# A decoder block's feed-forward entry: h2's evacuation split between ScalarE and VectorE, Silu's table loaded earlier, two sums moved from POOL to VectorE and placed later

## The chip, the cores and the metric

The kernel runs on one core of a Trainium2 chip. The metric is the device time of one execution in microseconds (us), the median of several runs. Engines are named as in the profile: PE is the matmul engine, DVE is VectorE, ACT is ScalarE, POOL is GpSimd, SP is the engine whose queue issues the DMAs.

## What is computed

The reference is one decoder block over 512 tokens of width 1024: two attention mixers, a merge through `w_out`, then a gated feed-forward network. Only its end is touched here:

```
x  = x + gt1 * (merged @ w_out)
h2 = rms_norm(x, norm2_gain) * (1.0 + sc2) + sh2
x  = x + gt2 * ((silu(h2 @ ffn_w_gate) * (h2 @ ffn_w_up)) @ ffn_w_down)
```

`sc2`, `sh2`, `gt1` and `gt2` are rows of `silu(c) @ ada_w + ada_b`. The feed-forward width is 2816, that is 22 columns of 128. All is in float32.

## The kernel before, in words

**Precision.** Each matmul operand is split in a high half (rounded to the matmul's format by a copy on ACT, `hi_of`) and a low half (source minus high half, `lo_of`, on DVE unless another engine is named). A product is then three matmuls: high by high, high by low, low by high. A weight chunk of 128x1024 (`wchunk`) is one DMA into `raw`, one ACT instruction into `whi` and one DVE subtraction into `wlo`; each of these three has four buffers.

**Order.** The program is written as generators that are stepped in an order chosen by hand (`mix`, `steps`, `run`). A scheduler then fixes the queue of each engine when the kernel is built: among instructions whose inputs are ready in its timing model it takes the one that is written first. A queue is executed strictly in its order. The class `Paced` wraps each engine; while its `gate` is set, each of its instructions is also ordered behind the gate's instruction by the scheduler, without a semaphore. All instructions of the wrapped engines carry line 144 in the profile, so groups are told apart by their tiles.

**Around the change.** `out_pairs` (L1344) computes the second half of `w_out`, for two token tiles at a time; `use_o` (L1330) adds the result to the residual `x2` on DVE and squares it on ACT (`junk`). `make_h2(q)` (L1365) handles half `q` of the tokens, 256 of them: a row of small DVE instructions for the reciprocal root (`rsqrt`), the scaled rows `xs`, and then for each pair of the eight columns `k` of h2 four PE transposes into one PSUM bank `pt` (there are two such banks) and, per column, the scale and shift out of PSUM into `h2f`, the high half `h2h` and the low half `h2l`. The low halves of odd columns are on POOL.

`first_gate_up` (L1567) multiplies the first pair of weight columns: for each half of the tokens four slabs of 24 matmuls of 256 tokens, gate (`fg`), up (`fu`), gate, up; all four accumulators (`mm`, four PSUM banks) are held to the end. `make_h2(1)` is stepped between the slabs of the first half. Then `gu_finish` (L1430) applies Silu to the gate accumulators on ACT, and multiplies with the up ones on DVE. `finish_mid` (L1419) splits the result into `mh` and `ml` for the down projection.

The second pair of columns (`gate_up(2)`, L1551) is plain: two gate slabs and two up slabs of 24 matmuls of 512 tokens. From the third pair on the gate product is done with seven products of half size in place of eight (`seven_products`, accumulators `fx` and `fy`). These need sums and differences of blocks of h2, the tiles T1 to T4, each with a high and a low half, made once in `h2_sums` (L1445) in two steps `j`, and sums of weight blocks (`weight_sums`, L1466, tiles `s3` and `s24`) for every pair. T1 to T4 are built in place in `h2f`.

Between the slabs the last rows of `ada_w` are worked off in portions (`mods_gen`): a strip is loaded by SP into a single buffer and two multiply-adds on DVE (`macc`) consume it.

At the end of the entry the lines L1590 to L1597 stand in this order: two gate chunks of the second pair into the list `early`, `gu_finish`, the first step of the sums, one up chunk into `early`, the rest of the sums, `finish_mid` for the first pair. `plain` (L1544) takes its chunks from `early` while there are any.

Of the kernel before, what the change touches and what calls it, by code (L numbers as in the profile page):

```python
# [14 lines left out]
AF = mybir.ActivationFunctionType  # L15
ALU = mybir.AluOpType
# [4 lines left out]
P = 128  # L21
# [3 lines left out]
KD = D // P  # L25
# [89 lines left out]
def hybrid_block(ctx, tc, a, out):  # L115
# [42 lines left out]
    def hi_of(dst, src, scale=1.0):  # L158
        act.activation(out=dst, in_=src, func=AF.Copy, scale=scale)

    def lo_of(dst, src, hi, eng=None):
        (eng or dve).tensor_tensor(out=dst, in0=src, in1=f32v(hi), op=ALU.subtract)
# [13 lines left out]
    ones = cst.tile([P, P], F32, name="ones")  # L176
# [77 lines left out]
    def wchunk(src, parts, n, eng_lo=None, cut=1):  # L254
        raw = wp.tile([P, 1024], F32, name="raw", tag="raw")
        rv = raw[:, : parts * n].rearrange("p (a n) -> p a n", a=parts)
        sp.dma_start(out=rv, in_=src)
        h = wp.tile([P, 1024], F32R, name="whi", tag="whi")
        l = wp.tile([P, 1024], F32R, name="wlo", tag="wlo")
        m = parts * n // cut  # L260
        for i in range(cut):
            c = slice(i * m, (i + 1) * m)
            hi_of(h[:, c], raw[:, c])
            lo_of(l[:, c], raw[:, c], h[:, c], eng_lo)
        return (h[:, : parts * n].rearrange("p (a n) -> p a n", a=parts),
                l[:, : parts * n].rearrange("p (a n) -> p a n", a=parts))

    def rows(w, r0, parts, c0, n):
        return w[r0 : r0 + parts * P, c0 : c0 + n].rearrange("(a p) n -> p a n", p=P)
# [15 lines left out]
    def run(gen):  # L285
        for _ in gen:
            pass
# [25 lines left out]
    def mix(*pairs):  # L313
        todo = [[g, n, 0] for g, n in pairs if n]
        while todo:
            best = min(todo, key=lambda e: (e[2] + 0.5) / e[1])
            if next(best[0], "end") == "end":
                todo.remove(best)
            else:
                best[2] += 1  # L320
                yield
# [22 lines left out]
    def gemm_tok(A, w, kt, c0, n, consume, tag="", eng_lo=None):  # L344
        ps = [mm.tile([P, S], F32, name=f"g{tag}{t}", tag="mm") for t in range(NT)]
        for k0 in range(0, kt, 2):
            parts = min(2, kt - k0)
            h, l = wchunk(rows(w, k0 * P, parts, c0, n), parts, n, eng_lo)
            for i in range(parts):
                k = k0 + i  # L350
                for t in range(NT):
                    ah, al = A(k, t)
                    pe.matmul(ps[t][:, :n], ah, h[:, i, :], start=(k == 0), stop=False)
                    pe.matmul(ps[t][:, :n], ah, l[:, i, :], start=False, stop=False)
                    pe.matmul(ps[t][:, :n], al, h[:, i, :], start=False, stop=(k == kt - 1))
            yield
        for t in range(NT):
            consume(t, ps[t][:, :n])
            yield
# [426 lines left out]
    def part(gen, n):  # L786
        for _ in range(n):
            if next(gen, "end") == "end":
                return
            yield  # L790
# [169 lines left out]
    mods_gen = mods()  # L960
# [369 lines left out]
    def use_o(c):  # L1330
        cs = slice(c * S, (c + 1) * S)

        def f(t, ps):
            tm = hp2.tile([P, S], F32, name="tm", tag="tm", bufs=2)
            dve.tensor_tensor(out=tm, in0=ps, in1=gt[4][:, cs], op=ALU.mult)
            dve.tensor_tensor(out=x2[t][:, cs], in0=x2[t][:, cs], in1=tm, op=ALU.add)
            junk = hp2.tile([P, S], BF16, name="junk", tag="junk", bufs=2)
            act.activation(out=junk, in_=x2[t][:, cs], func=AF.Square, accum_out=s2[:, c, t : t + 1])
        return f
# [25 lines left out]
    def make_h2(q):  # L1365
        need_mod(3)
        ts = slice(2 * q, 2 * q + 2)
        tcol = slice(2 * q * P, (2 * q + 2) * P)
        v = s2[:, 0, ts]
        dve.tensor_tensor(out=v, in0=v, in1=s2[:, 1, ts], op=ALU.add)  # L1370
        dve.tensor_scalar(out=v, in0=v, scalar1=1.0 / D, scalar2=EPS, op0=ALU.mult, op1=ALU.add)
        rsqrt(r2[:, ts], v, hp2, f"x2{q}")
        xs = [hp2.tile([P, D], F32, name="xs", tag="xs", bufs=4) for _ in range(2)]
        for t in (2 * q, 2 * q + 1):
            if t % 2 == 0:
                dve.tensor_scalar(out=xs[t % 2], in0=x2[t], scalar1=r2[:, t : t + 1], scalar2=None, op0=ALU.mult)
            else:
                act.activation(out=xs[t % 2], in_=x2[t], func=AF.Copy, scale=r2[:, t : t + 1])
        yield
        for k0 in range(0, KD, 2):  # L1380
            pt = tp.tile([P, 2, 2, P], F32, name="pt", tag="tp")
            for i in range(2):
                for j in range(2):
                    pe.transpose(pt[:, i, j, :], xs[j][:, (k0 + i) * P : (k0 + i + 1) * P], ident)
            for i in range(2):
                k = k0 + i
                h2 = h2f[k // 2][:, k % 2, tcol]
                dve.tensor_scalar(out=h2, in0=pt[:, i].rearrange("p a b -> p (a b)"), scalar1=modc[:, 3, k : k + 1],
                                  scalar2=modc[:, 2, k : k + 1], op0=ALU.mult, op1=ALU.add)
                hi_of(h2T[k][0][:, tcol], h2)  # L1390
                lo_of(h2T[k][1][:, tcol], h2, h2T[k][0][:, tcol], pool if k % 2 else dve)
            yield

    wo = gemm_tok(mA, a["w_out"][0], KD, 0, S, use_o(0), tag="wo0")
    steps(wo, 2)
    need_mod(4)
# [22 lines left out]
    def finish_mid(f0, sg, up=None):  # L1419
        mh = midp.tile([P, 2, S], F32R, name="mh", tag="mh")  # L1420
        ml = fp.tile([P, 2, S], F32R, name="ml", tag="ml", bufs=4)
        for i in [slice(0, 2)] if up is None else range(2):
            if up is not None:
                dve.tensor_tensor(out=sg[:, i], in0=sg[:, i], in1=up[i], op=ALU.mult)
            hi_of(mh[:, i], sg[:, i])
            lo_of(ml[:, i], sg[:, i], mh[:, i])
        for i in range(2):
            mid[f0 + i] = (mh[:, i], ml[:, i])
# [16 lines left out]
    def h2_sums():  # L1445
        def both(nm):
            return [h2s.tile([P, 4, 256], F32R, name=f"{nm}{e}") for e in "hl"]

        T1, T2, T3, T4 = (both(f"T{i}") for i in range(1, 5))
        for j in range(2):  # L1450
            b1, b2 = h2f[j], h2f[2 + j]
            jj = slice(2 * j, 2 * j + 2)
            dve.tensor_tensor(out=b1[:, :, LO], in0=b1[:, :, HI], in1=b1[:, :, LO], op=ALU.subtract)
            split_into([v[:, jj] for v in T1], b1[:, :, LO])
            pool.tensor_tensor(out=b1[:, :, HI], in0=b2[:, :, HI], in1=b1[:, :, HI], op=ALU.subtract)
            dve.tensor_tensor(out=b2[:, :, HI], in0=b2[:, :, HI], in1=b1[:, :, LO], op=ALU.subtract)
            split_into([v[:, jj] for v in T2], b2[:, :, HI])
            pool.tensor_tensor(out=b2[:, :, LO], in0=b2[:, :, LO], in1=b2[:, :, HI], op=ALU.subtract)
            split_into([v[:, jj] for v in T4], b2[:, :, LO])
            split_into([v[:, jj] for v in T3], b1[:, :, HI])  # L1460
            yield
        sums.update(T1=T1, T2=T2, T3=T3, T4=T4)
# [76 lines left out]
        dve.tensor_tensor(out=g[:, 1, LO], in0=A, in1=d, op=ALU.add)  # L1539
        yield g  # L1540

    early = []

    def plain(nm, w, f0):  # L1544
        ps = {(nm, i): mm.tile([P, S], F32, name=f"f{nm}{i}", tag="mm") for i in range(2)}
        for k0 in range(0, KD, 4):
            hl = early.pop(0) if early else wchunk(rows(w, k0 * P, 4, f0 * P, 256), 4, 256)
            gu_matmuls(ps, nm, k0, hl, slice(0, S), True)
            yield ps

# [36 lines left out]
    h2s = ctx.enter_context(tc.tile_pool(name="h2s", bufs=1, reuse_waits="tile"))  # L1587
    fp = ctx.enter_context(tc.tile_pool(name="fp", bufs=1, side="right", reuse_waits="tile"))
    strip_src["pool"] = fp
    for k0 in range(0, KD, 4):  # L1590
        early.append(wchunk(rows(wg, k0 * P, 4, 2 * P, 256), 4, 256))
    sg_first = gu_finish(0, ps_first)
    sums_gen = h2_sums()
    next(sums_gen)
    early.append(wchunk(rows(wu, 0, 4, 2 * P, 256), 4, 256))
    run(sums_gen)
    finish_mid(0, sg_first)  # L1597

    def store(c, t, ps):
        cs = slice(c * S, (c + 1) * S)  # L1600
# [33 lines left out]
    for i, (f0, f1) in enumerate(parts):  # L1634
        for f in range(f0, f1, 2):
            if f > 0:
                run(mix((gate_up(f), 6), (part(mods_gen, 4), 4)))
        if i == 0:
            run(mods_gen)
            need_mod(5)  # L1640
        down(f0, f1, i == len(parts) - 1)
# [25 lines left out]
```

## Time and profile before

| what | value |
|---|---|
| median of 3 runs | 907.83 us (907.36 to 909.1) |
| the profiled execution | 906.09 us |
| its span in the profile | 904.0 us |
| PE busy | 855.2 us, 95% |
| DVE busy | 636.0 us, 70% |
| ACT busy | 432.4 us, 48% |
| POOL busy | 176.3 us, 20% |
| granted clock of PE, mean | 0.983 of full speed; 1.00 from 490 us on |

The span is what the trace covers; the time is measured around it. Starts in the rows are us from the start of the span. A timeline row has the start, the duration, the engine, the line, the operation, the tile it writes and those it reads, the count, and in brackets the idle time of the engine before it with what ended that. Instructions of one engine overlap a little, so starts of neighbours are closer together than their durations.

### The profile page before, as it was taken

What the parts mean: (1) busy time and instruction counts of PE and PEld (TensorE: products, weight loads), DVE (VectorE), ACT (ScalarE), POOL (GpSimd) and SP (SyncE); (2) the same over time, 40 slices, a digit from 0 to 9 for tenths busy, and PEclk for the clock granted to TensorE, in tenths of its full rate; (3) what the DMA queues carried; (4) which work ended last, traced back from release to release, by engine and by line L of the source; (5) the groups of instructions that cost most, each with busy time, mean ns of one, the idle gap of its engine ahead of it and who ended that gap; (6) DMA issues with size and microseconds to landing.
All of it is one profiled execution on the core that took longest, in us unless ns stands there. A gap on an engine that the chain in (4) does not pass through costs nothing.

```text
span 904.0 us, 13055 instructions
## 1 busy us (share of the span) xinstructions
PE 855.2 (95%) x4676; PEld 731.4 (81%) x4676; DVE 636.0 (70%) x1288; ACT 432.4 (48%) x863; POOL 176.3 (20%) x222
## 2 busy tenths in 40 slices
PE   5999899899999997999999989999999999999997
PEld 4879899677777786787777878888899889988986
DVE  5857786778976788578779898866754565555644
ACT  5335654787764644466654345341344224431440
POOL 0003335434432037231148014000000000000000
PEclk9999999999999999699999999999999999999999
DMA  9934445321100654135488671553233313342312
GB/s 317 303 98 130 138 140 140 82 71 46 49 12 24 213 150 140 58 106 152 154 293 287 213 229 43 168 163 94 69 106 121 103 53 112 94 119 91 94 47 94
DMA packets 98116, 115.48 MB, mean 128 GB/s; under 512 B 6548, under 2 KB 70660, under 8 KB 98052
## 3 DMA queue, kind: packets, MB, share of 16 engines
q1 hardware_dynamic: 97956, 114.62, 41.3%
q8 instruction: 37, 0.61, 0.3%
q14 instruction: 27, 0.22, 0.1%
q10 hardware_dynamic: 96, 0.03, 0.0%
HBM read 106.24 MB, written 8.39 MB: 127 GB/s over the span
## 4 chain that ended last, share of the span: by engine, by line
PE 73%; DVE 13%; DMA 7%; ACT 2%; issue 2%; SPq 1%; POOL 1%; DVEq 0%; POOLq 0%; ACTq 0%
PE d L144 14%; PE fu L144 13%; PE gp L144 9%; PE fx L144 6%; PE ga L144 5%; PE fy L144 4%; PE pt L144 4%; PE av L144 3%; DMA raw<-in_ada_w_dram 3%; PE fg L144 3%; PE wa L144 2%; DVE macc L144 2%; PE gwo L144 2%; DVE wlo L144 2%; PE ps L144 2%
## 5 line engine op out<-in xcount | busy, mean ns | idle before, releaser
L144 ACT ACTIVATE whi<-raw 128x1024 fp32r<-128x1024 f32 (+4 forms) x162 | 142.1, 892 | 183.0 <-PE d L144 57.8
L144 DVE TENSOR_TENSOR wlo<-raw,whi 128x1024 fp32r<-128x1024 f32 (+3 forms) x122 | 144.0, 1184 | 73.5 <-ACT whi L144 73.1
L144 PE MATMUL fu<-h2l,whi 128*128 128x512 f32 (+1 forms) x192 | 71.3, 372 | 0.0
L144 PE MATMUL fu<-h2h,whi 128*128 128x512 f32 (+1 forms) x192 | 70.7, 372 | 0.0
L144 PE MATMUL fu<-h2h,wlo 128*128 128x512 f32 (+1 forms) x192 | 69.9, 373 | 0.0
L144 PE MATMUL d<-whi,mh 128*128 128x512 f32 x176 | 69.8, 398 | 0.0
L144 PE MATMUL d<-wlo,mh 128*128 128x512 f32 x176 | 69.6, 395 | 0.0
L144 PE MATMUL d<-whi,ml 128*128 128x512 f32 x176 | 67.0, 394 | 0.0
L144 ACT ACTIVATE s<-s,mn 128x384 f32<-128x384 f32 (+2 forms) x96 | 52.5, 548 | 23.0 <-DVE mn L144 22.3
L144 DVE TENSOR_TENSOR plo<-pt,phi 128x512 fp32r<-128x512 f32 (+2 forms) x78 | 46.1, 601 | 21.5 <-ACT phi L144 21.1
L144 POOL TENSOR_TENSOR wlo<-raw,whi 128x512 fp32r<-128x512 f32 x40 | 52.3, 1329 | 44.4 <-ACT whi L144 44.4
L144 PE MATMUL gp<-hTh,whi 128*128 128x512 f32 x128 | 55.4, 433 | 3.7 <-ACT qn L144 3.7
L144 ACT ACTIVATE phi<-pt 128x512 fp32r<-128x512 f32 (+2 forms) x78 | 40.1, 526 | 31.8 <-PE pt L144 31.4
L144 PE MATMUL gp<-hTh,wlo 128*128 128x512 f32 x128 | 52.0, 406 | 0.0
L144 PE MATMUL gp<-hTl,whi 128*128 128x512 f32 x128 | 51.6, 404 | 0.0
L144 DVE SCALAR_TENSOR_TENSOR macc<-raw,csil,macc 128x512 f32<-128x512 f32 x45 | 37.1, 829 | 8.8 <-DMA raw<-in_ada_w_dram 8.3
L144 PEld LDWEIGHTS fu<-h2l,whi 128*128 128x128 f32 x192 | 36.2, 189 | 6.1
L144 PEld LDWEIGHTS fu<-h2h,whi 128*128 128x128 f32 x192 | 35.9, 189 | 6.0
L144 PEld LDWEIGHTS fu<-h2h,wlo 128*128 128x128 f32 x192 | 35.6, 189 | 5.5
L144 PEld LDWEIGHTS d<-whi,mh 128*128 128x128 f32 x176 | 33.0, 188 | 8.2 <-issue 0.2
L144 PEld LDWEIGHTS d<-whi,ml 128*128 128x128 f32 x176 | 33.0, 188 | 8.1
L144 PEld LDWEIGHTS d<-wlo,mh 128*128 128x128 f32 x176 | 33.0, 188 | 7.9 <-issue 0.2
(427 smaller groups left out, 2427.6 us busy)
## 6 DMA issues: line engine op xcount, KB each, us to landing
raw<-in_ada_w_dram SPq DMA_DIRECT2D x26, 512.0 KB, 4.3
raw<-in_ffn_w_gate_dram SPq DMA_DIRECT2D x22, 512.0 KB, 4.7
raw<-in_ffn_w_up_dram SPq DMA_DIRECT2D x22, 512.0 KB, 3.8
raw<-in_ffn_w_down_dram SPq DMA_DIRECT2D x22, 512.0 KB, 4.9
araw<-in_ada_w_dram SPq DMA_DIRECT2D x32, 256.0 KB, 6.3
raw<-in_w_in_dram SPq DMA_DIRECT2D x16, 512.0 KB, 3.9
spill<-gs SPq DMA_DIRECT2D x24, 256.0 KB, 2.0
raw<-in_w_in_dram SPq DMA_DIRECT2D x12, 352.0 KB, 3.2
```

What stands on the lines that cost most here:

```text
L144: out = call(*args, **kw)
```

## The change

Four edits, all between `w_out` and the third pair of weight columns.

In `make_h2` an even column's high half is written by ACT straight from PSUM (Identity with scale and bias columns), while DVE writes its float32 value from the same bank; an odd column's float32 value is written by ACT from PSUM and its high half copied from that. All low halves are on DVE.

Ahead of `w_out` a Silu of one column is put on ACT, ordered behind ACT's last instruction so far, the last high half of the merged rows `mTh`.

In `h2_sums` the two subtractions per step that were on POOL are on DVE. Its two steps no longer follow `gu_finish`: they stand behind the first and second slab of the second pair, and DVE and ACT may take them only behind that slab's last matmul. The call of `finish_mid` for the first pair follows the third slab, and the portions of `mods_gen` of this pair come after it.

The list `early` is gone: the second pair's chunks are made where its slabs use them.

```
@@ -1385,12 +1385,21 @@
             for i in range(2):
                 k = k0 + i
                 h2 = h2f[k // 2][:, k % 2, tcol]
-                dve.tensor_scalar(out=h2, in0=pt[:, i].rearrange("p a b -> p (a b)"), scalar1=modc[:, 3, k : k + 1],
-                                  scalar2=modc[:, 2, k : k + 1], op0=ALU.mult, op1=ALU.add)
-                hi_of(h2T[k][0][:, tcol], h2)
-                lo_of(h2T[k][1][:, tcol], h2, h2T[k][0][:, tcol], pool if k % 2 else dve)
-            yield
-
+                src = pt[:, i].rearrange("p a b -> p (a b)")
+                a2, b2 = modc[:, 3, k : k + 1], modc[:, 2, k : k + 1]
+                hi, lo = (v[:, tcol] for v in h2T[k])
+                if i == 0:
+                    act.activation(out=hi, in_=src, func=AF.Identity, scale=a2, bias=b2)
+                    dve.tensor_scalar(out=h2, in0=src, scalar1=a2, scalar2=b2, op0=ALU.mult, op1=ALU.add)
+                else:
+                    act.activation(out=h2, in_=src, func=AF.Identity, scale=a2, bias=b2)
+                    hi_of(hi, h2)
+                lo_of(lo, h2, hi)
+            yield
+
+    act.gate = act.last
+    act.activation(out=warm, in_=ones[:, 0:1], func=AF.Silu)
+    act.gate = None
     wo = gemm_tok(mA, a["w_out"][0], KD, 0, S, use_o(0), tag="wo0")
     steps(wo, 2)
     need_mod(4)
@@ -1452,10 +1461,10 @@
             jj = slice(2 * j, 2 * j + 2)
             dve.tensor_tensor(out=b1[:, :, LO], in0=b1[:, :, HI], in1=b1[:, :, LO], op=ALU.subtract)
             split_into([v[:, jj] for v in T1], b1[:, :, LO])
-            pool.tensor_tensor(out=b1[:, :, HI], in0=b2[:, :, HI], in1=b1[:, :, HI], op=ALU.subtract)
+            dve.tensor_tensor(out=b1[:, :, HI], in0=b2[:, :, HI], in1=b1[:, :, HI], op=ALU.subtract)
             dve.tensor_tensor(out=b2[:, :, HI], in0=b2[:, :, HI], in1=b1[:, :, LO], op=ALU.subtract)
             split_into([v[:, jj] for v in T2], b2[:, :, HI])
-            pool.tensor_tensor(out=b2[:, :, LO], in0=b2[:, :, LO], in1=b2[:, :, HI], op=ALU.subtract)
+            dve.tensor_tensor(out=b2[:, :, LO], in0=b2[:, :, LO], in1=b2[:, :, HI], op=ALU.subtract)
             split_into([v[:, jj] for v in T4], b2[:, :, LO])
             split_into([v[:, jj] for v in T3], b1[:, :, HI])
             yield
@@ -1539,12 +1548,10 @@
         dve.tensor_tensor(out=g[:, 1, LO], in0=A, in1=d, op=ALU.add)
         yield g
 
-    early = []
-
     def plain(nm, w, f0):
         ps = {(nm, i): mm.tile([P, S], F32, name=f"f{nm}{i}", tag="mm") for i in range(2)}
         for k0 in range(0, KD, 4):
-            hl = early.pop(0) if early else wchunk(rows(w, k0 * P, 4, f0 * P, 256), 4, 256)
+            hl = wchunk(rows(w, k0 * P, 4, f0 * P, 256), 4, 256)
             gu_matmuls(ps, nm, k0, hl, slice(0, S), True)
             yield ps
 
@@ -1587,14 +1594,13 @@
     h2s = ctx.enter_context(tc.tile_pool(name="h2s", bufs=1, reuse_waits="tile"))
     fp = ctx.enter_context(tc.tile_pool(name="fp", bufs=1, side="right", reuse_waits="tile"))
     strip_src["pool"] = fp
-    for k0 in range(0, KD, 4):
-        early.append(wchunk(rows(wg, k0 * P, 4, 2 * P, 256), 4, 256))
     sg_first = gu_finish(0, ps_first)
     sums_gen = h2_sums()
-    next(sums_gen)
-    early.append(wchunk(rows(wu, 0, 4, 2 * P, 256), 4, 256))
-    run(sums_gen)
-    finish_mid(0, sg_first)
+
+    def gated_sums():
+        dve.gate = act.gate = pe.last
+        next(sums_gen, None)
+        dve.gate = act.gate = None
 
     def store(c, t, ps):
         cs = slice(c * S, (c + 1) * S)
@@ -1634,7 +1640,13 @@
     for i, (f0, f1) in enumerate(parts):
         for f in range(f0, f1, 2):
             if f > 0:
-                run(mix((gate_up(f), 6), (part(mods_gen, 4), 4)))
+                slabs = gate_up(f)
+                if f == 2:
+                    for _ in range(3):
+                        next(slabs)
+                        gated_sums()
+                    finish_mid(0, sg_first)
+                run(mix((slabs, 6), (part(mods_gen, 4), 4)))
         if i == 0:
             run(mods_gen)
             need_mod(5)
```

## Rows read from the trace of the kernel before

**Rows 1.** Waits of PE, 490 us to the end: total, times, longest.
```profile
PE fg L144 <- DVE h2l L144: 2.4, 2, 2.2
PE fg L144 <- ACT sg L144: 1.9, 1, 1.9
PE pt L144 <- DVE h2f L144: 1.7, 1, 1.7
```

**Rows 2.** Windows; columns: stretch, length, then busy us of each engine.
```profile
561.70:586.00 24.30, 22.38 (x100) 18.36 (x99) 19.88 (x25) 10.83 (x14) 2.21 (x1) 1.00 0.62 189
586.00:904.00 318.00, 313.37 (x1720) 271.15 (x1718) 184.83 (x253) 104.89 (x138) 0.00 (x0) 1.00 0.32 97
```

**Rows 3.** Timeline of PE: start, duration, group, [idle before it <-releaser].
```profile
536.70 0.39 PE L144 MATMUL fg<-h2l,whi 128*128 128x256 f32 x1 [2.24 <-DVE h2l L144]
...
559.28 0.28 PE L144 MATMUL fg<-h2h,wlo 128*128 128x256 f32 x1
...
563.63 0.50 PE L144 MATMUL fg<-h2h,whi 128*128 128x512 f32 x1 [1.92 <-ACT sg L144]
```

**Rows 4.** Timeline of VectorE, the first half of the tokens' h2.
```profile
531.77 1.89 DVE L144 TENSOR_SCALAR h2f<-pt,modc 128x256 f32<-128x256 f32 x4
...
534.57 1.74 DVE L144 TENSOR_TENSOR wlo<-raw,whi 128x1024 fp32r<-128x1024 f32 x1
536.23 0.41 DVE L144 TENSOR_TENSOR h2l<-h2f,h2h 128x256 fp32r<-128x256 f32 x1
```

**Rows 5.** Timeline of POOL, one of the sums.
```profile
559.27 1.74 POOL L144 TENSOR_TENSOR h2f<-h2f 128x512 f32<-128x512 f32 x1 [1.56 <-DVE h2f L144]
```

**Rows 6.** Tile wlo on VectorE, 561.7 to 586 us: min/median/max, first, last.
```profile
L144 DVE TENSOR_TENSOR wlo<-raw,whi x6: 1210/1214/2312, 559.8 to 580.5; 128x1024 fp32r<-128x1024 f32 x6
```

**Rows 7.** Tile h2f, whole run, the same columns.
```profile
L144 DVE TENSOR_SCALAR h2f<-pt,modc x16: 525/532/543, 531.8 to 553.2; 128x256 f32<-128x256 f32 x16
L144 ACT ACTIVATE h2h<-h2f x16: 400/418/422, 532.6 to 554.5; 128x256 fp32r<-128x256 f32 x16
...
L144 DVE TENSOR_TENSOR h2l<-h2f,h2h x8: 410/411/967, 536.2 to 557.0; 128x256 fp32r<-128x256 f32 x8
...
L144 POOL TENSOR_TENSOR h2f<-h2f x2: 1736/1975/2214, 559.3 to 563.4; 128x512 f32<-128x512 f32 x2
...
L144 DVE TENSOR_TENSOR T2l<-h2f,T2h x2: 680/1230/1781, 564.4 to 569.7; 128x512 fp32r<-128x512 f32 x2
```

**Rows 8.** Timeline of ScalarE, at three places.
```profile
497.80 1.06 ACT L144 ACTIVATE whi<-raw 128x1024 fp32r<-128x1024 f32 x1 [1.19 <-PE gwo L144]
...
530.38 1.06 ACT L144 ACTIVATE whi<-raw 128x1024 fp32r<-128x1024 f32 x1 [0.69 <-PE wo L144]
...
561.04 0.63 ACT L144 ACTIVATE T4h<-h2f 128x512 fp32r<-128x512 f32 x1 [1.18 <-POOL h2f L144]
561.69 1.28 ACT L144 ACT_TABLE_LOAD   x1
```

**Rows 9.** Groups of ScalarE by form, whole run: busy us, mean ns | idle.
```profile
L144 ACT ACTIVATE h<-px,modc 128x512 f32<-128x512 f32 x7 | 5.4, 771 | 6.3 <-DVE modc L144 6.3
...
L144 ACT ACTIVATE m<-fx 128x256 f32<-128x256 f32 x9 | 3.4, 381 | 2.4 <-PE fx L144 2.4
...
L144 ACT ACTIVATE X<-pt 64x512 f32<-64x512 f32 x4 | 2.3, 587 | 0.0
```

**Rows 10.** Timeline of VectorE, a transposed bank read by two engines.
```profile
76.06 1.41 DVE L144 COPY X<-pt 64x511 f32<-64x511 f32 x2 [0.37 <-ACT X L144]
```

**Rows 11.** Chain of waits: start, us, what (with its matmuls).
```profile
542.24 2.88 PE fg L144 x24
...
563.63 11.17 PE fg L144 x48
```

**Rows 12.** Groups of VectorE by form, 561.7 to 586 us.
```profile
L144 DVE SCALAR_TENSOR_TENSOR macc<-strip,csil,macc 128x512 f32<-128x512 f32 x4 | 3.0, 744 | 2.6 <-DMA strip<-in_ada_w_dram 2.6
```

**Rows 13.** Waits of the DMA queue SP, 536 to 563 us.
```profile
SPq L935 <- DVE macc L144: 18.3, 1, 18.3
```

## The prediction, made before the change was run

> **What bounds it now.** First the waits of the matmul engine (PE) from 490 us to the end [rows 1]: three kinds only, 6.0 us in all. The windows show what follows [rows 2]: after 586 us PE is busy for 313.4 of 318.0 us, and none of those waits lies there, so time saved ahead of 586 us should reach the end. The timeline of PE gives the places [rows 3]: a first hole of 1.7 us, where transposes of h2 wait for VectorE to empty their bank; 2.2 us at 536.70, where the first matmuls wait for a low half of h2; 0.2 us at the second half of the tokens; and 1.9 us at 563.63, where the second pair of weight slabs needs a bank that Silu still has to read. No gain can exceed these 6.0 us by much.
>
> What stands behind each: in the timeline of VectorE (DVE) [rows 4] the four tensor_scalars that empty the transposes take 1.89 us from 531.77; then, among others, a weight's low half of 1.74 us passes, and only at 536.23 comes the low half of h2 that PE wants. That wait is an order of DVE's queue, and length too: while POOL works [rows 5], DVE's two-input instructions stretch. The weight subtraction is 1.21 us at best and 2.31 at worst [rows 6], the 256-column one of h2 0.41 to 0.97 [rows 7]. The hole of 1.9 us belongs to ScalarE (ACT) [rows 8]: fg was complete near 559.5 us [rows 3], yet ACT stood in its queue before a sum's high half, T4h, which waited for POOL's 1.74 us subtraction [rows 5], and then loaded Silu's table for 1.28 us.
>
> **Part one, h2's evacuation.** Per pair of columns before: DVE two tensor_scalars (0.53 us each) and one low half (0.41), ACT two copies (0.42 each), POOL one low half [rows 7]. After: ACT two Identity reads of PSUM and one copy; DVE one tensor_scalar and two low halves, 0.53 + 0.41 + 0.41 = 1.35 us against 1.47. A 256-column Identity with column scale and bias is not in the trace. Bounds: 0.38 us (256-column Copy out of PSUM) and 0.77 us (the Identity at 512 columns) [rows 9]. A Copy out of PSUM costs 0.21 us less at 256 columns than at 512, so I take 0.77 - 0.21, about 0.55 us (estimate). ACT: 0.55 + 0.55 + 0.42 = 1.52 us a pair.
>
> The new wait: both engines read one transposed bank. In [rows 10] VectorE's copy out of pt idled 0.37 us until ScalarE's copies were done, though the two share nothing but the source bank. So I let readers take turns: 0.55 + 0.53 + 0.55 = 1.63 us per bank, where DVE alone took 0.95 (half of 1.89). There are two banks, so part of it is hidden. The Trainium skill's page "PSUM — Partial Sum Buffer", section "PSUM bank collisions raise a hardware error", says that two engines must never access one quadrant of a bank at once, reads against reads included. That speaks against this sharing, and the row agrees; with a bank free to both the chain would be 1.10 us.
>
> First column: a weight's high half frees ACT at 531.4 [rows 8]; Identity to 532.0, tensor_scalar to 532.5, low half to 533.0, in place of 536.7. PE needs 0.72 us per column (2.88 us for four [rows 11]), and pairs come at about 1.5 us (ACT's 1.52 above): one more pause of some 0.5 us. Holes one and two, 3.9 us, become about 2.4 (1.8 and 0.5): a gain of 1.5 us. Bounds: 2.2 us if nothing pauses after 533.0; minus 0.5 if ACT's queue puts other work in between. Hole three goes with POOL's stretch: 0.1 us (0 to 0.2).
>
> **Part two, Silu's table.** The load moves behind the last high half of mT. The weight's high half that follows on ACT begins at 497.80 after 1.19 us of idle [rows 8]; load and dummy (about 1.5 us) delay it by 0.3 us, and no wait of PE in [rows 1] is on such a weight there, so it costs nothing; if that cover fails, 0.3 us. It was 1.28 of hole four; the rest was POOL's T4, which part three moves. Silu can then start while fu's last 2.2 us of matmuls still run. I take 1.9 us as gained; at the least 1.3 (the table alone).
>
> **Part three, the sums.** Four 512-column subtractions leave POOL (two of them 1.98 us each) for DVE at 0.68 us [rows 7], and all sums start later, in the queues of ACT and DVE behind the first and the second slab of the second weight pair. Nobody needs them before the first seven-product matmul (fx) at 586 us. Queued behind them on DVE are the first mid tile, the ada multiply-adds and the third pair's weight sums, for which fx waits. DVE is busy 19.9 of the 24.3 us from 561.7 to 586 [rows 2]. Take off the 5.2 us of sums in it (T3l, two T2l, two T4l and a subtraction at 0.68, and T2l's stretch of 1.1 [rows 7]), add sixteen operations at 0.68 = 10.9, take off the weight's stretch of 1.1 [rows 6]: 24.5 us wanted, where the window without its hole is 22.4. Of that two multiply-adds (1.5 us [rows 12]) and the third weight slot's low half (1.2) are wanted only after fx starts, and a weight's low half (1.2) moves ahead of 561.7, into the place of the sums: about 20.6. It fits, narrowly, and fx starts on time: 0, with bounds 0 and 5.4 us (rival B).
>
> **Part four, the weights fetched early.** The list with the second gate slab and the first up chunk goes. Their slots wait for the same releases as before; what changes is their rank, now behind the first Silu. Cost 0 if DVE does their low halves before PE wants them, up to 1.9 (rival C). On the DMA queue (SP) a strip of ada_w waits 18.3 us for a multiply-add on DVE [rows 13], with the third pair's weights behind it; they come earlier if DVE is freer ahead of 561.7, later if not, and that is in B's price.
>
> **Sum.** 1.5 + 0.1 + 1.9 + 0 = 3.5 us. The profiled execution took 906.09 us (span 904.0 and 2.1 around it), 1.74 us less than the median of the runs, 907.83. From the median: 904.3 us; the profiled execution would read 902.6.
>
> **Rivals.** A: the bank's turns and two strict queues lock step. A pair then costs 0.55 + 0.53 + 0.55 + 0.42 + 0.41 = 2.46 us, two pairs from 531.4 end at 536.3, about where the matmuls get going now: holes one and two stay, the gain is 2.0, and the time 905.8. For it: [rows 10]. Against: two banks, and columns that can be used singly. Chance 0.15.
>
> B, slower: DVE becomes the bound before fx. The second half of the sums may not start until two slabs, 11.2 us [rows 11], after the entry; 11.2 us are left, for 5.4 of sums, 1.2 of mid, three weight lows (3.6), four weight sums of 0.68 (2.7) and four multiply-adds (3.0): 15.9, or 4.7 too many, and with one operation left of the first half 5.4. PE stalls at fx; past 3.5 us the change loses, and at 5.4 it gives 909.7. Against: weight sums can run before the sums start, and the window's work fits in total. Chance 0.13.
>
> C: hole four only changes its owner. The gate slab's low half started at 559.8 and took the 2.31 us [rows 6], so it ended 0.4 us into the hole; ranked later it may fill it. The gain is then 1.6: 906.2 us. Against: the sums that ran before it are gone from both engines. Chance 0.12.
>
> **Numbers.** Forecast 0.60. A measurement tells 0.2% (1.8 us) from no change: faster is below 906.0, slower above 909.6. Faster: 0.60 and half of A, 0.68. Same: the rest of A, C and a little of B, 0.20. Slower: 0.12. The range runs from 901.9 (all holes shut) to 907.9, past A and C, and leaves out B and a thin tail.
>
> **What would show it.** Right: no POOL work after 530 us; the table load near 497 us and none before the Silu; hole four gone; the first low half of h2 within 3 us of the transposes; fx 3.5 us earlier with no new wait of PE. Wrong: waits for h2h or h2l of over 3 us in all; fg waiting for wlo (C); fx or fy waiting for wlo or a T tile (B); PE waiting for macc.

## The result, and the profile after

The changed kernel took 902.65 us (median of 7 runs, 900.99 to 904.26) beside 907.38 for the kernel before on the same chip: a ratio of 0.9946, 95% interval 0.993 to 0.9963, faster by 4.7 us. The profiled execution took 903.17 us with a span of 901.4, where that of before took 906.09 with 904.0. Timed twice more, the same kernel gave 905.62 (ratio 0.9976, 0.9962 to 0.9991) and 903.20 (0.9946, 0.9925 to 0.9966). Against the median of before in the same timing these are gains of 4.7, 2.4 and 5.2 us. So the median of one kernel moves by up to 3 us from one timing to the next, and what the parts do has to be read from stretches of the profile.

Three stretches carry it: from the first transpose of h2 to the first matmul of the second weight pair (the entry), from there to the first `fx`, and the rest. The windows of before, cut there (columns as in [rows 2]):

```profile
530.18:563.63 33.45, 27.41 (x225) 26.52 (x223) 29.38 (x55) 17.61 (x33) 12.37 (x12) 1.00 0.27 83
563.63:585.98 22.35, 22.35 (x98) 18.34 (x99) 17.93 (x22) 8.89 (x12) 1.96 (x1) 1.00 0.61 184
```

The same of after, and two short windows in its entry:

```profile
529.81:561.12 31.31, 28.52 (x226) 28.08 (x224) 20.32 (x49) 18.42 (x35) 0.00 (x0) 0.95 0.36 119
561.12:583.36 22.24, 22.24 (x100) 18.24 (x99) 21.40 (x31) 11.12 (x16) 0.00 (x0) 1.00 0.49 143
583.36:901.40 318.04, 313.39 (x1720) 271.16 (x1718) 185.31 (x254) 104.76 (x138) 0.00 (x0) 1.00 0.31 96
534.40:537.00 2.60, 2.60 (x17) 2.60 (x18) 2.57 (x13) 1.44 (x4) 0.00 (x0) 0.71 0.82 271
537.00:539.00 2.00, 2.00 (x12) 2.00 (x12) 1.33 (x6) 1.84 (x4) 0.00 (x0) 0.52 0.70 256
```

The entry is 2.14 us shorter, the second stretch 0.11, the rest as long as before (318.02 there). In the entry, length less PE's busy time is idle time: 6.04 us before, 2.79 after. PE's busy time, though, grew by 1.11 us, because the granted clock was 0.71 over the 2.6 us from 534.40 and 0.52 over the next two, next to the lower level of 1.2 GHz (0.50); before it was 1.00 throughout. So 3.25 us of waits went and 1.11 came back as slower matmuls.

The waits of PE from 490 us on, after (of [rows 1], `fg` for `sg` is gone, and `fg` for `h2l` too):

```profile
PE pt L144 <- ACT h2f L144: 2.1, 1, 2.1
PE fg L144 <- ACT h2h L144: 0.7, 1, 0.7
```

The timeline of PE at the first h2 columns, after (before, the holes were 1.7 and 2.2 us [rows 1]):

```profile
531.57 0.51 PE L144 MATMUL fg<-h2h,whi 128*128 128x256 f32 x2 [0.73 <-ACT h2h L144]
...
534.37 0.66 PE L144 MATMUL pt<-ident,xs 128*128 128x128 f32 x4 [2.06 <-ACT h2f L144]
...
538.17 0.41 PE L144 MATMUL fg<-h2l,whi 128*128 128x256 f32 x1
538.38 0.41 PE L144 MATMUL fg<-h2h,wlo 128*128 128x256 f32 x1
...
539.11 0.29 PE L144 MATMUL fg<-h2h,whi 128*128 128x256 f32 x1
539.23 0.28 PE L144 MATMUL fg<-h2l,whi 128*128 128x256 f32 x1
```

Starts are 0.21 us apart at 538 and 0.12 at 539: that is the clock. The wait of 2.06 us is explained by two queues. VectorE, after:

```profile
530.85 1.28 DVE L144 TENSOR_TENSOR x<-x,tm 128x512 f32<-128x512 f32 x2
532.04 1.22 DVE L144 TENSOR_TENSOR wlo<-raw,whi 128x1024 fp32r<-128x1024 f32 x1
533.18 0.99 DVE L144 TENSOR_SCALAR h2f<-pt,modc 128x256 f32<-128x256 f32 x2
```

ScalarE, after, at Silu's table, at the first h2 columns and at the Silu itself:

```profile
496.25 1.28 ACT L144 ACT_TABLE_LOAD   x1
497.54 0.20 ACT L144 ACTIVATE warm<-ones 128x1 f32<-128x1 f32 x1
497.65 1.05 ACT L144 ACTIVATE whi<-raw 128x1024 fp32r<-128x1024 f32 x1
...
530.97 1.00 ACT L144 ACTIVATE h2h<-pt,modc 128x256 fp32r<-128x256 f32 x2
531.87 0.63 ACT L144 ACTIVATE junk<-x 128x512 bf16<-128x512 f32 x1
...
533.76 1.02 ACT L144 ACTIVATE h2f<-pt,modc 128x256 f32<-128x256 f32 x2 [0.56 <-DVE h2f L144]
...
559.04 0.60 ACT L144 ACTIVATE sg<-fg 128x512 f32<-128x512 f32 x1 [2.54 <-PE fg L144]
```

ScalarE has its first high halves done by 532.0. The tensor_scalars of the same banks begin only at 533.18, behind the residual adds of the last two token tiles and a weight's low half; ScalarE's odd columns, which read the bank after VectorE, begin at 533.76; PE can refill the bank at 534.37. The table's load now lies near 496; the weight's high half behind it starts at 497.65 (497.80 in [rows 8]). Counted from the first matmul of `w_out` (479.10 us, before 479.44) that is 0.2 us later, and no wait of PE came of it. The Silu at 559.04 follows its accumulator directly.

### The profile page after: what moved, and what is told of

Read it like the earlier page. It is cut to its first block, busy times and chain, and to the rows that moved or that the text cites. A ratio compares the mean times of both kernels' runs of the same rounds, so it can differ in the third digit from the quotient of the medians.

```text
span 901.4 us, 13041 instructions
## 1 busy us (share of the span) xinstructions
PE 854.4 (95%) x4676; PEld 731.8 (81%) x4676; DVE 632.3 (70%) x1292; ACT 436.9 (48%) x872; POOL 161.4 (18%) x210
## 4 chain that ended last, share of the span: by engine, by line
PE 70%; DVE 14%; DMA 7%; ACT 3%; issue 2%; POOL 2%; SPq 1%; DVEq 0%; ACTq 0%; POOLq 0%
PE d L144 14%; PE fu L144 13%; PE gp L144 9%; PE fx L144 6%; PE ga L144 5%; PE fy L144 4%; PE pt L144 4%; PE av L144 3%; DMA raw<-in_ada_w_dram 3%; DVE macc L144 3%; PE fg L144 3%; DVE wlo L144 2%; PE ps L144 2%; DVE s L144 1%; PE wa L144 1%
## 5 line engine op out<-in xcount | busy, mean ns | idle before, releaser
L144 ACT ACTIVATE s<-s,mn 128x384 f32<-128x384 f32 (+2 forms) x96 | 52.5, 548 | 22.4 <-DVE mn L144 21.9
```

The costliest lines, as they stand in the source:

```text
L144: out = call(*args, **kw)
```

## The experiments

All numbers by stretch are from one profiled execution each. "Idle" is the entry's length less PE's busy time in it, and "f2 to fx" is the second stretch, from the second weight pair to the first `fx`. Each ratio is to the kernel before, timed beside it on the same chip. The changed kernel alone gave 0.9946 and 0.9976, so ratios that lie no further apart do not rank these kernels.

PE's busy time varies by 0.5 us between kernels with the clock at 1.00 (26.95 to 27.47), so a difference of that size in it says nothing about the clock.

| kernel | entry, us | PE busy | idle | clock | f2 to fx | DVE busy there | ratio to before (95%) |
|---|---|---|---|---|---|---|---|
| before | 33.45 | 27.41 | 6.04 | 1.00 | 22.35 | 17.93 | 1 |
| changed | 31.31 | 28.52 | 2.79 | 0.95 | 22.24 | 21.40 | 0.9946 (0.993 to 0.9963) |
| changed, second time | 32.68 | 29.62 | 3.06 | 0.90 | 22.25 | 20.90 | 0.9976 (0.9962 to 0.9991) |
| changed, third time | 31.66 | 28.52 | 3.14 | 0.95 | 22.24 | 21.18 | 0.9946 (0.9925 to 0.9966) |
| without the early Silu | 31.99 | 28.53 | 3.46 | 0.95 | 22.24 | 21.79 | 0.9937 (0.9916 to 0.9957) |
| old evacuation | 31.24 | 26.95 | 4.29 | 1.00 | 22.25 | 22.25 | 0.995 (0.993 to 0.9971) |
| old sums | 32.01 | 28.77 | 3.24 | 0.95 | 22.24 | 17.26 | 0.9969 (0.9949 to 0.9989) |
| early Silu alone | 32.14 | 27.41 | 4.73 | 1.00 | 22.35 | 18.79 | 0.9988 (0.9973 to 1.0002) |
| late sums alone | 31.50 | 26.97 | 4.53 | 1.00 | 22.25 | 22.25 | 0.9929 (0.9901 to 0.9957) |
| new evacuation alone | 30.27 | 27.23 | 3.04 | 1.00 | 22.24 | 17.88 | 0.9945 (0.9924 to 0.9966) |
| two gates | 29.00 | 27.46 | 1.54 | 1.00 | 22.28 | 22.28 | 0.9913 (0.9886 to 0.994) |
| two gates, second time | 29.00 | 27.47 | 1.53 | 1.00 | 22.24 | 22.18 | 0.993 (0.9907 to 0.9953) |

**The changed kernel again**, unaltered.

> The changed kernel again, unaltered. Main theory (M): only the entry changed; three holes of 3.6 us are shut, and in the profiled execution 1.3 us of that was lost because the matmuls from 535.5 to 538.9 us ran at the lower granted clock. So executions without that dip gain 3.6 us, with it 2.3: ratio to before 0.996 to 0.9975. Rival (R): something outside the entry got faster as well; then the ratio is 0.9946 again (4.9 us) and the executions differ ahead of 480 us or behind 586 us.

Idle time agreed (3.06 and 2.79 us), the clock did not (0.90 and 0.95), and with it the entry, by 1.4 us. Its ratio was 0.9976, and 0.9946 again in the third timing: by the time alone the two readings are not told apart. By the profile only the entry is shorter; the rest after `fx` took 318.28 us, no less than before's 318.02.

**Without the early Silu.**

```
-    act.gate = act.last
-    act.activation(out=warm, in_=ones[:, 0:1], func=AF.Silu)
-    act.gate = None
```

> The changed kernel without the early Silu. M: the table load then stands directly ahead of the first Silu, where ScalarE now idles 2.5 us waiting for fg, so the 1.28 us hide there: no difference to the changed kernel within 0.3 us, and no hole of PE at the first slab of the second pair. Rival, as the prediction counted it (1.28 us of the hole are the load): the hole is back with 1.3 us and the time is 1.3 us above the changed kernel.

The load came back into the entry, and cost nothing. The entry is 0.7 us longer than the changed kernel's all the same, but by another wait, that of `pt` for `h2f`: 2.7 us here, 2.1, 2.3 and 2.4 in the three executions of the changed kernel. Its timeline of ScalarE:

```profile
554.55 1.28 ACT L144 ACT_TABLE_LOAD   x1
557.08 0.60 ACT L144 ACTIVATE sg<-fg 128x512 f32<-128x512 f32 x1 [1.24 <-PE fg L144]
```

After the load ScalarE still idles 1.24 us until `fg` is done. In the changed kernel the early Silu is worth nothing.

**The old evacuation** in the changed kernel.

```
-                if i == 0:
-                    act.activation(out=hi, in_=src, func=AF.Identity, scale=a2, bias=b2)
...
+                dve.tensor_scalar(out=h2, in0=src, scalar1=a2, scalar2=b2, op0=ALU.mult, op1=ALU.add)
+                hi_of(hi, h2)
+                lo_of(lo, h2, hi, pool if k % 2 else dve)
```

> The changed kernel with the old evacuation of h2 (two tensor_scalars on VectorE, odd low halves on POOL). M: the two holes ahead of 537 us come back with 3.9 us in place of 2.8, so 1.1 us slower than the changed kernel if neither execution has the clock dip; if the dip belongs to the new evacuation's longer single idle, it does not show here and the two come out equal in the profile. The hole at the second pair stays shut. Rival (lock step, A of the prediction): the new evacuation gains nothing, difference 0.

Its timeline of PE has both old holes:

```profile
533.51 0.63 PE L144 MATMUL pt<-ident,xs 128*128 128x128 f32 x4 [2.04 <-DVE h2f L144]
...
537.30 0.38 PE L144 MATMUL fg<-h2l,whi 128*128 128x256 f32 x1 [2.26 <-DVE h2l L144]
```

Idle time rose by 1.5 us against the changed kernel, but the clock stayed at 1.00, and the entry came out equal (31.24 and 31.31): what the new evacuation wins in waits, it loses again in PE's busy time (28.52 in place of 26.95). Of that 1.6 us, 1.1 to 1.3 are the clock, if kernels with the new evacuation at a clock of 1.00 (27.23 to 27.47) are the measure; the rest is not explained.

**The old sums**, with the list `early`, in the changed kernel.

```
-            dve.tensor_tensor(out=b1[:, :, HI], in0=b2[:, :, HI], in1=b1[:, :, HI], op=ALU.subtract)
+            pool.tensor_tensor(out=b1[:, :, HI], in0=b2[:, :, HI], in1=b1[:, :, HI], op=ALU.subtract)
...
+    next(sums_gen)
+    early.append(wchunk(rows(wu, 0, 4, 2 * P, 256), 4, 256))
+    run(sums_gen)
+    finish_mid(0, sg_first)
```

> The changed kernel with the sums where and on which engines they were, and the early chunks back. M: the hole at the second pair returns without the table load: ScalarE still queues T4h, which waits for POOL, ahead of the Silu; 0.6 us of hole, and 0.6 to 0.9 us above the changed kernel. Rival: the queue before the Silu simply shifts and the whole 1.9 us return.

The hole stayed shut, against both readings. ScalarE in it, at the place of the last of [rows 8]:

```profile
557.64 0.61 ACT L144 ACTIVATE T4h<-h2f 128x512 fp32r<-128x512 f32 x1
559.43 0.60 ACT L144 ACTIVATE sg<-fg 128x512 f32<-128x512 f32 x1 [1.18 <-PE fg L144]
```

The likely reason, not tried by itself, is that POOL has no low halves of h2 between its sums any more. Its first subtraction for T4:

```profile
555.74 1.69 POOL L144 TENSOR_TENSOR h2f<-h2f 128x512 f32<-128x512 f32 x1 [1.22 <-DVE h2f L144]
```

That is 26.7 us after the first transpose (529.02); before it was 29.1 (559.27 in [rows 5], 530.18). So T4h is done before `fg` is.

**Each part alone**, on the kernel before: the three lines of the early Silu; the late sums with the list gone; the new evacuation. The edits are those of the change.

> The kernel before with the early Silu alone. ScalarE still queues the T4h that waits for POOL ahead of the Silu. Prediction's account: the hole of 1.92 us at the second pair shrinks by the load, 1.28, to 0.6 us; the stretch from the transposes to the second pair is 32.2 us (before 33.45). Rival: something else ends the wait 1.3 us later and nothing is gained.

> The kernel before with the sums on VectorE and late, nothing else. M: the table load stands ahead of the Silu, but ScalarE reaches it 1.5 us before fg is complete, so the hole is 0 to 0.3 us; the stretch is 31.2 to 31.6 us, as with the early Silu added (31.24 in the run without the new evacuation). Rival: the load is on the path and the stretch is 32.5.

> The kernel before with the new evacuation of h2 alone. M: holes one and two shrink from 3.9 to about 3.0 us and the clock falls behind them (0.90 to 0.95 over the stretch), which costs 1.3 to 2.6 us: no gain there. With POOL free of low halves T4h is done by 558.3, so the hole at the second pair is small even with the table load (0.3 us). Stretch 32 to 33 us, ratio to before 0.997 to 1.0. Rival: the evacuation alone gains the 1.5 us of the prediction and keeps the clock; stretch below 31.5.

The early Silu alone took 1.31 us from the entry (its own load is 1.28) and left this, in the timeline of PE:

```profile
565.40 0.50 PE L144 MATMUL fg<-h2h,whi 128*128 128x512 f32 x1 [0.50 <-ACT sg L144]
```

Its time fell by less than the measurement tells (the interval reaches 1.0002); that execution also has a wait of 1.4 us behind the first `fx`, for ScalarE's `m`. ScalarE was waiting for `gu` there, and VectorE, which makes `gu`, had waited for a strip of `ada_w`:

```profile
588.84 1.54 DVE L144 SCALAR_TENSOR_TENSOR macc<-strip,csil,macc 128x512 f32<-128x512 f32 x2 [2.92 <-DMA strip<-in_ada_w_dram]
```

The late sums alone shut the hole wholly with the load still in place; idle time fell by 1.51 only, as the first hole was 2.3 us in that execution. The new evacuation alone shut it too, and took 1.1 us more from the other holes (3.04 idle against 6.04, of which 1.9 are the fourth). Its waits are those of the changed kernel, yet, against the expectation, its clock did not fall and its entry is the shorter by 1.0 us. Its timeline of PE:

```profile
535.52 0.50 PE L144 MATMUL fg<-h2h,whi 128*128 128x256 f32 x2 [0.73 <-ACT h2h L144]
...
538.57 0.66 PE L144 MATMUL pt<-ident,xs 128*128 128x128 f32 x4 [2.31 <-ACT h2f L144]
```

So any one part removes the fourth hole, wholly or for the most part. The causes stood in a row in ScalarE's queue, and each part alone moves the Silu forward by about as much as the hole was long; their gains do not add up, and together they are worth the hole's 1.9 us. Which half of the late sums does it without the new evacuation, the place or the engine, was not tried.

**Two gates.** Behind the changed kernel's first two evacuated banks (`h2_mark[0, 2]` is the last instruction of ScalarE and VectorE on the second pair of columns), two things are ordered that stood ahead of it: the entry's fourth weight chunk (its second up slab), and the last two residual adds with their squares.

```
+            act.gate, dve.gate = h2_mark.get((0, 2), (None, None))
             dve.tensor_tensor(out=x2[t][:, cs], in0=x2[t][:, cs], in1=tm, op=ALU.add)
...
+            h2_mark[q, k0] = act.last, dve.last
...
+                        if (nm, k0) == ("u", 4):
+                            act.gate, dve.gate = h2_mark[0, 2]
...
```

(Behind each of the two places both gates are set back to None.)

> The changed kernel with h2's first evacuation ahead in the queues: the last residual adds, their squares and the fourth weight chunk of the first pair are ordered behind the first two column pairs. Theory (M2): the hole of 2.1 to 2.7 us exists because VectorE's tensor_scalar stands behind two adds and that weight, and the clock falls after it; with them behind, that wait is under 0.8 us, PE's granted clock stays at 1.00 from the transposes to the second pair, and this stretch takes 29.0 us (+-0.5) in place of 31.3 to 32.7: 2.5 to 3.5 us faster than the changed kernel. Rival (R2): the two readers of one bank and the strict queues set the pace; then the wait stays over 1.5 us and the stretch over 30.5. A further rival: the clock falls all the same, since PE waits a little several times; stretch 30 to 31.

The timeline of PE in the gated kernel:

```profile
533.07 0.50 PE L144 MATMUL fg<-h2h,whi 128*128 128x256 f32 x2 [0.33 <-ACT h2h L144]
...
534.25 0.66 PE L144 MATMUL pt<-ident,xs 128*128 128x128 f32 x4 [0.44 <-ACT h2f L144]
```

That of its VectorE:

```profile
533.05 1.00 DVE L144 TENSOR_SCALAR h2f<-pt,modc 128x256 f32<-128x256 f32 x2
...
535.67 1.29 DVE L144 TENSOR_TENSOR x<-x,tm 128x512 f32<-128x512 f32 x2
536.88 1.22 DVE L144 TENSOR_TENSOR wlo<-raw,whi 128x1024 fp32r<-128x1024 f32 x1
```

That of its ScalarE:

```profile
532.46 1.02 ACT L144 ACTIVATE h2h<-pt,modc 128x256 fp32r<-128x256 f32 x2 [1.24 <-PE pt L144]
533.63 1.02 ACT L144 ACTIVATE h2f<-pt,modc 128x256 f32<-128x256 f32 x2 [0.15 <-DVE h2f L144]
```

The adds and the low half now follow the tensor_scalars. No wait is over 0.44 us, the clock is 1.00, and the entry is 29.00 us: 4.45 less than before, 2.3 less than in the changed kernel. The two gates were not tried singly.

**Two gates beside the changed kernel**, on one chip.

> The two gates behind h2's third bank (weight's low and high half, residual adds) repeated beside the changed kernel on one chip, since the two had been timed on different ones. Theory (the waits at the first matmuls on h2, and the clock that fell behind them, are the order of the queues of DVE and ACT): transposes to first f2 matmul 29.0 to 29.4 us, granted clock 1.00 there, no wait of PE over 0.5 us between the transposes and 586 us, and about 3 us faster than the changed kernel of this call, near 0.991 to 0.992 of the kernel before. Rival (the earlier low time was that execution's luck): stretch 31 us or more, clock below 1.00, and no difference from the changed kernel beyond 1 us.

> The changed kernel unaltered, beside the one with two gates. Both theories: 0.994 to 0.998 of the kernel before, the stretch from the transposes to the first f2 matmul 31.2 to 32.7 us with the granted clock at 0.90 to 0.95 in it, f2 to fx 22.2 to 22.3 us without a wait. If the clock stays at 1.00 here, its fall is chance and not the order of the queues.

The entry was 29.00 us against 31.66, the clock 1.00 against 0.95. The medians were 901.90 and 903.20, 1.3 us apart, with intervals that overlap: the profile shows the gain, the timing does not, and the 3 us that were expected did not come. By the profile it is the best kernel of this study; its ratios of 0.9913 and 0.993 are not clear of the 0.9929 of the late sums alone.

**The sums one slab later**, one execution.

```
                 if f == 2:
+                    next(slabs)
                     for _ in range(3):
                         next(slabs)
```

> The changed kernel with the sums of h2 one slab later (5.5 us). Theory (the second pair's 22.2 us are nearly all DVE's, 21.4 busy, and T2's and T4's low halves are done some 4.5 us before they are read): with a slab of 5.5 us more the first fx and fy matmuls wait, 0.5 to 2 us of new waits of PE on T tiles or on the weight sums; f2 to fx 22.2 to 24 us, or the wait just behind the first fx. Rival (the sums are far from binding): no wait on them, f2 to fx 22.2 to 22.3, time unchanged.

There was no new wait but 0.2 us on ScalarE's `m`. From the second pair to `fx` it took 22.24 us, with VectorE busy for 20.29 of it, and 903.39 us in all. That is the rival's side: the sums are not binding where the change puts them.

**The late sums with two subtractions per step back on POOL**, one execution.

```
-            dve.tensor_tensor(out=b2[:, :, LO], in0=b2[:, :, LO], in1=b2[:, :, HI], op=ALU.subtract)
+            pool.tensor_tensor(out=b2[:, :, LO], in0=b2[:, :, LO], in1=b2[:, :, HI], op=ALU.subtract)
```

(And the same for `b1[:, :, HI]`.)

> The changed kernel with the two subtractions per step of h2's sums given back to POOL, at their late place. Theory (what shut hole four is the place of the sums and the new evacuation; the engine does not matter there, and DVE has 0.8 us to spare with them): hole four stays shut; POOL takes about 2.0 us per subtraction, DVE's two-input instructions that overlap it stretch, DVE busy between f2 and fx 18.5 to 21, f2 to fx 22.2 to 22.4; time outside the span 2.1 us if POOL's work decides that, 1.8 if not. Rival (POOL's slower subtraction makes T2 or T4 late): PE waits for a T tile or a weight sum, 0.5 to 2 us at fx or fy.

It took 910.76 us: slower, as the rival had it, and by more, but the wait is not at a T tile. The rest after `fx` took 325.12 us, 7.1 more. Its timeline of POOL:

```profile
571.98 4.60 POOL L144 TENSOR_TENSOR h2f<-h2f,h2f 128x512 f32<-128x512 f32 x1 [2.63 <-DVE h2f L144]
```

Of PE, in the second weight block of the third pair:

```profile
591.58 0.58 PE L144 MATMUL fx<-h2h,whi 128*128 128x256 f32 x1 [4.27 <-ACT m L144]
```

Of VectorE ahead of that:

```profile
589.25 0.75 DVE L144 SCALAR_TENSOR_TENSOR macc<-strip,csil,macc 128x512 f32<-128x512 f32 x1 [1.42 <-DMA strip<-in_ada_w_dram]
589.91 0.68 DVE L144 TENSOR_TENSOR gu<-gu,fu 128x512 f32<-128x512 f32 x1
```

And of ScalarE:

```profile
590.63 0.63 ACT L144 ACTIVATE mh<-gu 128x512 fp32r<-128x512 f32 x1 [2.07 <-DVE gu L144]
591.16 0.37 ACT L144 ACTIVATE m<-fx 128x256 f32<-128x256 f32 x1
```

POOL's subtraction took 4.60 us, VectorE came late to `gu`, a multiply-add that waited 1.42 us for its strip stood in front of that, and ScalarE stood in its queue at `mh` before the `m` that PE wanted. How much of this is POOL's is open: with the early Silu alone a wait for a strip led to the same wait for `m`, 1.4 us, with the sums at their old place. Of the 7.1 us, 4.3 are that wait; PE's busy time grew by 2.8 (316.21 in place of 313.39), since the clock fell behind the wait as well, as its window shows:

```profile
590.00:595.00 5.00, 3.42 (x16) 3.42 (x17) 4.80 (x7) 2.12 (x4) 0.00 (x0) 0.56 0.31 100
```

## Why the prediction was right, and where it was not

The time lay in the range and on the forecast's side: 4.7 us less where 3.5 were forecast. The steps did less well than that, and the agreement in size is in part luck: the two repeats gave 2.4 and 5.2. In the profile the entry and the second stretch gave 2.25 us; 0.32 more lie outside the span (2.09 us around it before, 1.77 after); and 0.37 ahead of the entry, where the start of `w_out` varies from 476.6 to 482.6 us between executions with the same code up to there. These make up the 2.9 us between the two profiled executions. The rest of the 4.7 is no stretch of a profile, and stays open: before's only profiled execution was 1.7 us faster than the median the prediction was given, while that of the changed kernel was 0.5 slower than its own.

**Part one** was put at 1.5 us for the first two holes and 0.1 for the third. The waits shrank from 4.1 us (1.7 and 2.4) to 2.8, so 1.3, near it; but the clock took 1.1 back, and 2.2 in the second execution (busy 29.62). Net it is 0.2 or less. The forecast waits were 1.8 us before the first matmul and 0.5 behind it (2.3 in all, not 2.4); they were 0.73 and 2.06. The step that failed is "Identity to 532.0, tensor_scalar to 532.5": the Identities ended there, the tensor_scalar began at 533.18. The prediction had seen a weight's low half in VectorE's queue [rows 4] and moved it behind the tensor_scalar without saying what would do so; its bound named ScalarE's queue as the one that might put work in between, and it was VectorE's. The gated kernel, in which that order holds, comes to 29.00 us. Two of the prediction's own signs failed with it: the first low half of h2 began 4.35 us after the first transpose and 3.3 after the last (534.16), where 3 were allowed, and `fx` came 2.6 us earlier (583.36 for 585.98) where 3.5 were forecast. The durations were right: an Identity of 256 columns took 0.56 us (0.55 taken), and the readers take turns (Identity at 532.46, tensor_scalar at 533.05, Identity at 533.63 in the gated kernel). The Trainium skill's page "PSUM — Partial Sum Buffer", section "PSUM bank collisions raise a hardware error", has it that two engines must not read one quadrant of a bank at once; the rows agree.

**That the clock falls** was in no term and no rival. In seven of the eight profiled executions with the new evacuation and no gates it fell in or behind the two waits, in none of the four with the old evacuation, in none of the two gated ones.

**Parts two and three** were to give 1.9 us, and the hole of 1.9 us went. The split was wrong: 1.28 for the table and the rest for T4h hold only if the table is taken away first. Alone the Silu shortened the entry by 1.31 us and the sums by 1.95 (idle time by 1.51), and with either the sums or the new evacuation in place the Silu gives nothing. Part one alone shut the hole too, which the prediction did not have.

**The sums on VectorE** cost 0, as said. VectorE was busy 21.40 us of 22.24 (about 20.6 of 22.4 estimated). The busy share looked narrow and was not: the last T2l ends at 584.1 and is first read at 588.2, and a slab later they still cost nothing.

**Rival A**, the lock step, gave the right kind of wait (`pt` for ScalarE's `h2f`, behind VectorE's read of the bank), but in the gated kernel, which takes the same turns, that wait is 0.44 us at the most; what is above that was queue order. **Rival B**, VectorE late before `fx`, did not happen with the sums on VectorE, and a loss of that size came when two of them were on POOL at the late place: 910.76, where B had 909.7. Its path was another one, `gu` and `m` in place of the weight sums. **Rival C** did not occur: `fg` waits for no `wlo` there.

## What to carry to other kernels

When an evacuation is split over two engines that take turns at a bank, its speed is that of the slower queue: list what stands in each queue between the two reads, and order it behind them, before counting the instructions saved. When a hole has several causes in a row on one queue, price each alone and again with the others gone; one cheap edit may be worth all of them. And a wait of PE may cost twice, once as idle time and once as slower matmuls behind it: compare PE's busy time over the same matmuls, not the waits alone.

## What was not expected of the hardware

The clock fell or not behind nearly the same waits: 0.73 and 2.06 us with a fall to 0.52, 0.73 and 2.31 without one. Before's holes of 1.7 and 2.2 us had none either. In the seven executions with a fall it came in the second wait three times, and four times only when PE was at work again. What decides it was not tried, so two gated executions without a fall do not prove that the gates prevent it.

The time outside the span was 2.1 us before and with the early Silu alone, and 1.8 in every other kernel, with POOL at work in the late sums or not. No run here explains these 0.3 us.

POOL's subtractions of 512 columns took 1.49 to 2.21 us before (the two longer are in [rows 7]), and one of them 4.60 us at the late place, beside VectorE at work. VectorE's instructions within those 4.60 us kept their 0.68 and 1.21 us; beside POOL's next one, of 1.30 us, a subtraction of VectorE took 1.77.
